# Two 1024x1024 products as seven half-size products each, from sums of operand quadrants

## The chip, the cores and the metric

The kernel runs on one core of one Trainium2 chip. The metric is the device time of one execution in microseconds (us), the median of several executions. In the profile PE is TensorE (the matmuls), PEld its weight loads, DVE is VectorE, ACT is ScalarE, POOL is GpSimd and SP is the engine from whose queue nearly all DMAs are issued.

## The reference, cut to what matters

One layer of an encoder on 1024 tokens of width 1024. Four mixers (a linear recurrence, neighbourhood attention, a state-space model and a pooling mixer) give four branches of width 512; the change touches what comes behind them, the last two 1024x1024 products.

```python
ys = jnp.stack([y_a, y_b, y_c, y_d], axis=2).astype(x.dtype)
gates = jax.nn.sigmoid(merge.reshape(bsz, s, N_BRANCH, D_MODEL))
merged = jnp.sum(jnp.einsum('bsnw,nwd->bsnd', ys, w_branch[i]) * gates, axis=2)
x = x + (merged @ w_out[i]).astype(x.dtype)
x = x + jax.nn.sigmoid(x @ ple_gate[i]) * (p[i] @ ple_proj[i])
```

All of `merged`, `w_out`, `x` and `ple_gate` are 1024x1024 in float32. `p @ ple_proj` is computed early and lies in DRAM as `pp`.

## The kernel before

Every large product is made of three matmuls per block: an operand is split into a high part H (a ScalarE copy, rounded to the type fp32r) and a low part L = operand - H (a VectorE subtraction), and H·H + H·L + L·H are summed in PSUM (`split`, L83; `mm3`, L87, whose three matmuls are L92 to L94). One matmul has a 128x128 stationary and a 128x512 moving operand. A 1024x1024x1024 product therefore takes 8 (contraction chunks) x 8 (token tiles) x 2 (column halves) x 3 = 384 matmuls.

The order on each engine is made by a scheduler when the kernel is built; at run time each engine works through its own queue in that order, and an instruction that waits holds up all that stand behind it on that engine. DMAs of the SP queue are issued in order too.

`merge` (L1174) goes through the four branches in the order 1, 0, 2, 3. For each branch it makes 8 row tiles m of 128 features by 1024 tokens, each in two halves of 512 tokens (PSUM tiles `ps_s` and `ps_o`, two buffers each). VectorE multiplies the PSUM half by the gate (`mgt`, read from DRAM, four buffers) and adds it to the accumulator `acc` (two instructions of 128x512). In the last branch the sum goes back into `mgt`, and whenever a row tile is complete it is split into `mH` and `mL`, which lie where the normed input lay.

`final` (L1200) then runs four blocks: two column halves of the product with `w_out`, two of the product with `ple_gate`. Each block loads its weights (`wide_load`, two tiles `wr` of 1 MB), splits them (`wide_split`, four pieces of 128x1024) and makes 8 token tiles of 24 matmuls (`wide_product`, PSUM `ps_z`, two buffers). `put_x` adds the input to a token tile (`fx`), stores it to DRAM as `x1d`, transposes it with four matmuls against the identity (`ps_t`, L97), and splits it into `xH`, `xL`, the operand of the second product. `put_o` takes the sigmoid, multiplies by `pp`, adds `x1d` and stores the output.

Of the kernel before, what the change touches and what calls it, by code (L numbers as in the profile page):

```python
# [24 lines left out]
BANDS = (0, 8, 24, 32)  # L25
SC = (1.25, 1.35, 0.95)
VIDX = (0, 1, 1, 2)


class Kern:  # L30
# [308 lines left out]

    def norm_load(self, tmp, hf):  # L340
        if hf == 0:
            self.hnH = [self.big.tile([128, 1024], F32R, tag=f"bH{k}", name="hnH") for k in range(8)]
            self.hnL = [self.big.tile([128, 1024], F32R, tag=f"bL{k}", name="hnL") for k in range(8)]
# [167 lines left out]
    def at_units(self, ap, rd, qk, bias, vd):  # L511
# [9 lines left out]
        for g in range(2):  # L521
# [14 lines left out]
            for j in range(4):  # L536
# [597 lines left out]

    def y_split(self, yp, mp, n, out):

        hl = [[yp.tile([128, 1024], F32R, tag=f"my{k}{j}", name="my" + "HL"[j]) for j in range(2)]
              for k in range(4)]
        yield 0.0, 0.0
        for k in range(4):  # L1140
            y = mp.tile([128, 1024], F32, tag="mgt", name="my", bufs=4)
            self.nc.sync.dma_start(y, self.yd[n][k * 128:k * 128 + 128, :])
            if n == 1:
                g = mp.tile([128, 1024], F32, tag="mgt", name="myg", bufs=4)
                self.nc.sync.dma_start(g, self.sgd[1][k * 128:k * 128 + 128, :])
                self.mul(y, y, g)
            H, L = hl[k]
            self.split(H, L, y)
            out.append((H, L))
            yield 0.0, 2.0  # L1150
# [21 lines left out]
                    yield m, hf, gt, pb  # L1172

    def merge(self, mp, mq, order, Y):  # L1174
        acc = [self.big.tile([128, 1024], F32, tag=f"bH{k}", name="acc") for k in range(8)]
        self.mH, self.mL = [], []
        for a, n in enumerate(order):
            nxt = []
            pre = self.y_split((mp, mq)[(a + 1) % 2], mp, order[a + 1], nxt) if a < 3 else iter(())
            for m, hf, gt, pb in self.branch_products(mp, n, Y):  # L1180
                t = slice(hf * 512, hf * 512 + 512)
                if a == 0:
                    self.mul(acc[m][:, t], pb, gt[:, t])
                else:
                    self.mul(gt[:, t], pb, gt[:, t])
                    if a < 3:
                        self.add(acc[m][:, t], acc[m][:, t], gt[:, t])
                    else:
                        self.add(gt[:, t], acc[m][:, t], gt[:, t])
                        if hf:  # L1190
                            H, L = (self.big.tile([128, 1024], F32R, tag=f"b{c}{m}", name=f"m{c}") for c in "HL")
                            self.split(H, L, gt)
                            self.mH.append(H)
                            self.mL.append(L)
                if m >= 2 and hf:
                    next(pre, None)
            Y = nxt


    def final(self):  # L1200
        nc, i = self.nc, self.i
        x1d = self.dp.tile([S, D], F32, name="x1d")
        mH, mL = self.mH, self.mL
        with self.tc.tile_pool(name="fn", bufs=2, reuse_waits="tile") as fp:
            xH = fp.tile([128, 8, 1024], F32R, name="xH", bufs=1)
            xL = fp.tile([128, 8, 1024], F32R, name="xL", bufs=1)

            def put_x(nb, t, ps):
                cols, tk = slice(nb * 512, nb * 512 + 512), slice(t * 128, t * 128 + 128)
                x = fp.tile([128, 512], F32, tag="fx", name="fx", bufs=3)  # L1210
                nc.sync.dma_start(x, i["x"][tk, cols])
                yield
                self.add(x, x, ps())
                nc.sync.dma_start(x1d[tk, cols], x)
                pt = self.ps("t")
                for c in range(4):
                    self.tr(pt[:, c * 128:c * 128 + 128], x[:, c * 128:c * 128 + 128], 128)
                k = slice(nb * 4, nb * 4 + 4)
                self.split(xH[:, k, tk], xL[:, k, tk], pt.rearrange("p (c q) -> p c q", c=4))

            def put_o(nb, t, ps):
                cols, tk = slice(nb * 512, nb * 512 + 512), slice(t * 128, t * 128 + 128)
                o = fp.tile([128, 512], F32, tag="fx", name="fo", bufs=3)
                nc.sync.dma_start(o, x1d[tk, cols])
                pw = fp.tile([128, 512], F32, tag="fp", name="fp")
                nc.sync.dma_start(pw, self.pp[tk, cols])
                yield
                g = fp.tile([128, 512], F32, tag="fg", name="fg")
                self.act(g, ps(), AF.Sigmoid)
                self.mul(g, g, pw)  # L1230
                self.add(o, o, g)
                nc.sync.dma_start(self.out[0][tk, cols], o)

            self.fw = itertools.count()
            blocks = [(n, nb) for n in ("w_out", "ple_gate") for nb in range(2)]
            raws = [self.wide_load(*blocks[0])]
            for m, (n, nb) in enumerate(blocks):
                if m < 2:
                    self.wide_product(fp, [a[:, :] for a in mH], [a[:, :] for a in mL], raws[0], put_x, nb)
                else:  # L1240
                    self.wide_product(fp, [xH[:, k, :] for k in range(8)], [xL[:, k, :] for k in range(8)],
                                      raws[0], put_o, nb)
                raws = [self.wide_load(*blocks[m + 1])] if m < 3 else []

    def wide_load(self, n, nb):

        out = []
        for kh in range(2):
            r = self.wp.tile([128, 4, 512], F32, tag="wr", name="wr")
            self.nc.sync.dma_start(r, self.i[n][kh * 512:kh * 512 + 512, nb * 512:nb * 512 + 512]  # L1250
                                   .rearrange("(k p) n -> p k n", p=128))
            out.append(r)
        return out

    def wide_split(self, fp, raws):
        hl = []
        for q in range(4):
            if next(self.fw) % 5 < 3:
                H, L = self.whl([128, 2, 512])
            else:  # L1260
                H, L = (fp.tile([128, 2, 512], F32R, tag="fw" + c, name="w" + c) for c in "hl")
            self.split(H, L, raws[q // 2][:, q % 2 * 2:q % 2 * 2 + 2, :])
            hl += [(H[:, k, :], L[:, k, :]) for k in range(2)]
        return hl

    def wide_product(self, fp, aH, aL, raws, put, nb):

        hl = self.wide_split(fp, raws)
        box = [None]
        nxt = put(nb, 0, lambda: box[0])  # L1270
        next(nxt)
        for t in range(8):
            cur = nxt
            ps = self.ps("z")
            c = slice(t * 128, t * 128 + 128)
            self.mm3(ps, [(aH[k][:, c], aL[k][:, c]) + hl[k] for k in range(8)])
            if t < 7:
                nxt = put(nb, t + 1, lambda: box[0])
                next(nxt)
            box[0] = ps  # L1280
            next(cur, None)

    def run(self):
        tc = self.tc
        with tc.tile_pool(name="gzp", bufs=2, reuse_waits="tile") as self.gzp:
# [13 lines left out]
            with tc.tile_pool(name="mp", bufs=1, reuse_waits="tile") as mp:  # L1299
# [9 lines left out]
            self.final()  # L1309


def encoder_kernel(tc, ins, out):
# [33 lines left out]
```

## Time and profile before

| | |
|---|---|
| time before, median of 3 runs | 1386.07 us (1385.12 to 1386.26) |
| the profiled execution: its own time | 1385.52 us |
| the profiled execution: its span | 1383.7 us |
| busy TensorE, share of the span | 99% |
| busy VectorE | 61% |
| busy ScalarE | 38% |
| granted TensorE clock, mean | 0.999 |

The span is that of the instructions in the trace; the execution's own time has 1.82 us more around it. Positions in the program are given in us from the start of the span.

### The profile page before, as it was taken

To read this page: it belongs to the slowest core of one execution; us is meant where nothing else is said; L and a number is where in the kernel's file an instruction comes from. 1 tells how busy PE (TensorE), PEld (TensorE's weight loads), DVE (VectorE), ACT (ScalarE), POOL (GpSimd) and SP (SyncE) were. 2 spreads that over 40 slices of the span, in tenths; PEclk is the share of its full clock that TensorE was granted. 3 is DMA by queue.
4 is the path that set the end of the run, shared out by engine and by line. 5 is a ranking of instruction groups with operands and counts; after the bars stand their busy time and mean duration, and the time that the engine had idled before them with its cause. 6 is when DMAs were issued, how large, how long until landed. Compare 5 with 4: busy or idle time off the path is not lost.

```text
span 1383.7 us, 19208 instructions
## 1 busy us (share of the span) xinstructions
PE 1368.5 (99%) x7450; PEld 1159.6 (84%) x7450; DVE 843.8 (61%) x1592; ACT 521.3 (38%) x825; POOL 20.6 (1%) x81
## 2 busy tenths in 40 slices
PE   7999999999999999999999999999999999999998
PEld 6999998888788888788888888888888888888886
DVE  6551766455299797979757556636566767732332
ACT  6542676588332222222243662644312212211211
POOL 2200000000000000000000000000000000000000
PEclk9999999999999999999999999999999999999999
DMA  9451223433443142324264143135527655333543
GB/s 323 130 146 59 72 77 118 133 105 109 100 127 99 61 129 89 114 88 127 91 213 142 35 140 110 61 137 188 213 94 258 206 175 176 135 108 128 179 144 119
DMA packets 141054, 181.99 MB, mean 132 GB/s; under 512 B 29200, under 2 KB 100888, under 8 KB 140962
## 3 DMA queue, kind: packets, MB, share of 16 engines
q1 hardware_dynamic: 140610, 180.72, 40.4%
q8 instruction: 59, 0.97, 0.3%
q14 instruction: 33, 0.27, 0.1%
q0 software_dynamic: 352, 0.03, 0.0%
HBM read 127.05 MB, written 54.03 MB: 131 GB/s over the span
## 4 chain that ended last, share of the span: by engine, by line
PE 93%; DVE 5%; DMA 1%; ACT 1%; issue 0%; SPq 0%; DVEq 0%
PE ps_z L92 19%; PE ps_z L93 19%; PE ps_z L94 19%; PE ps_t L97 4%; PE ps_t L93 4%; PE ps_t L92 4%; PE ps_t L94 4%; PE ps_o L92 3%; PE ps_o L93 3%; PE ps_o L94 3%; PE ps_s L92 3%; PE ps_s L93 3%; PE ps_s L94 3%; PE ps_o L578 2%; PE ps_s L543 2%; PE ps_s L1068 1%
## 5 line engine op out<-in xcount | busy, mean ns | idle before, releaser
L92 PE MATMUL ps_z<-hnH,wh 128*128 128x512 f32 x744 | 293.2, 394 | 2.0 <-DVE bgt L58 2.0
L93 PE MATMUL ps_z<-hnL,wh 128*128 128x512 f32 x744 | 292.0, 392 | 0.0
L94 PE MATMUL ps_z<-hnH,wl 128*128 128x512 f32 x744 | 291.9, 392 | 0.0
L64 DVE TENSOR_TENSOR wl<-wr,wh 128x1024 fp32r<-128x1024 f32 x88 | 107.4, 1221 | 110.4 <-ACT wh L80 109.6
L92 PEld LDWEIGHTS ps_z<-hnH,wh 128*128 128x128 f32 x744 | 139.8, 188 | 30.8 <-DVE bgt L58 2.4
L94 PEld LDWEIGHTS ps_z<-hnH,wl 128*128 128x128 f32 x744 | 139.8, 188 | 28.5 <-issue 0.4
L93 PEld LDWEIGHTS ps_z<-hnL,wh 128*128 128x128 f32 x744 | 139.8, 188 | 27.9 <-issue 0.4
L80 ACT ACTIVATE wh<-wr 128x1024 fp32r<-128x1024 f32 x88 | 93.0, 1059 | 166.3 <-PE ps_z L93 81.2
L92 PE MATMUL ps_z<-wh,hnH 128*128 128x256 f32 x384 | 108.3, 285 | 0.5 <-ACT zqk L80 0.5
L94 PE MATMUL ps_z<-wh,hnL 128*128 128x256 f32 x384 | 108.5, 287 | 0.0
L93 PE MATMUL ps_z<-wl,hnH 128*128 128x256 f32 x384 | 108.1, 283 | 0.0
L93 PE MATMUL ps_t<-hnL,wh 128*128 128x512 f32 x216 | 84.2, 390 | 0.0
L92 PE MATMUL ps_t<-hnH,wh 128*128 128x512 f32 x216 | 84.1, 389 | 0.0
L94 PE MATMUL ps_t<-hnH,wl 128*128 128x512 f32 x216 | 84.0, 389 | 0.0
L92 PEld LDWEIGHTS ps_z<-wh,hnH 128*128 128x128 f32 x384 | 73.2, 192 | 1.2 <-ACT zqk L80 1.2
L93 PEld LDWEIGHTS ps_z<-wl,hnH 128*128 128x128 f32 x384 | 73.5, 191 | 0.0
L94 PEld LDWEIGHTS ps_z<-wh,hnL 128*128 128x128 f32 x384 | 72.9, 192 | 0.0
L94 PE MATMUL ps_z<-wh,mL 128*128 128x512 f32 x128 | 51.0, 399 | 0.0
L549 DVE CUSTOM_DVE_ANT_0 sc<-ps_s,bias 128x384 f32<-128x384 f32 x64 | 34.2, 554 | 27.2 <-PE ps_s L543 14.6
L92 PE MATMUL ps_o<-myH,wh 128*128 128x512 f32 x128 | 49.9, 390 | 0.4 <-DVE pm L67 0.4
L92 PE MATMUL ps_z<-wh,mH 128*128 128x512 f32 x128 | 50.2, 393 | 0.0
L93 PE MATMUL ps_z<-wl,mH 128*128 128x512 f32 x128 | 50.0, 391 | 0.0
(371 smaller groups left out, 2596.9 us busy)
## 6 DMA issues: line engine op xcount, KB each, us to landing
wr<-in_w_in_dram SPq DMA_DIRECT2D x32, 1024.0 KB, 5.3
gd<-gz SPq DMA_DIRECT2D x32, 512.0 KB, 2.9
mgt<-gd SPq DMA_DIRECT2D x32, 512.0 KB, 4.2
sg<-bgt SPq DMA_DIRECT2D x16, 512.0 KB, 3.1
my<-yd SPq DMA_DIRECT2D x16, 512.0 KB, 4.2
mbr<-in_w_branch_dram SPq DMA_DIRECT2D x8, 1024.0 KB, 6.7
bias<-E SPq DMA_DIRECT2D x128, 48.0 KB, 2.0
xt<-in_x_dram SPq DMA_DIRECT2D x8, 512.0 KB, 10.0
```

The lines of the kernel that those rows point to most:

```text
L64: self.nc.vector.tensor_tensor(out, a, b, ALU.subtract)
L80: return self.nc.scalar.activation(out, a, AF.Copy)
L92: mm(ps, aH, bH, start=(k == 0), stop=False)
L93: mm(ps, aH, bL, start=False, stop=False)
L94: mm(ps, aL, bH, start=False, stop=(k == n - 1))
L97: self.nc.tensor.transpose(ps, src, self.ident[:k, :k])
L543: nc.tensor.matmul(pss[h], q[h][:, qs], km[h][(slice(0, 128),) + ks], start=(p == 0), stop=(p == 1))
L549: nc.vector.tensor_tensor_reduce(sc, pss[h], bias[g][h][:, VIDX[j], :], 1.0, -3e38, ALU.add, ALU.max, mx)
L578: m = self.nc.tensor.matmul(po[64 * h:64 * h + 64, j * 128:j * 128 + 128], vb[:, g + c, j, h * 64:h * 64 + 64], PT[h][:, c * 128:c * 128 + ...
L1068: nc.tensor.matmul(py[:, c], Q[k][:, a, 1:9, :].rearrange("p t c -> p (t c)"), X[k][:, c], start=False, stop=(k == 1))
```

## The change

The two last products are computed by a seven-product scheme instead of the plain one. The left operand A (1024 tokens by 1024) and the weights B are cut into quadrants of 512x512. Seven products of 512x512x512 are made from sums and differences of quadrants, and the four quadrants of the result are sums of these seven. A half-size product has 4 (contraction chunks) x 4 (token tiles) x 3 = 48 matmuls of the same shape as before.

- `merge` no longer splits its result: the accumulator `m` (128x8x1024, float32) stays whole. At the start of the last branch the four quadrants of `w_out` (`wq`, 1 MB each) are loaded into the buffers from which the third branch read its left operand (`my`).
- `seven` runs the seven products. `prep` makes the operands of the next one while the present one runs: per half of the contraction a sum or difference of the left quadrants (into `stmp` or back into `m`), its split into `ah`, a difference of weight quadrants (in place), and its split into `wh`, `wl`. The numbers 1 to 7 are the keys of `plan`.
- Products 1, 6, 7 and 4 add up in one set of four PSUM tiles (X), 5 and 3 and then 2 in another (Z). After products 1, 6 and 5 ScalarE copies the sum so far to `snap` tiles in SBUF. After products 3, 7, 2 and 4 a quadrant of the result is complete: `put_x` or `put_o` adds the snapshot and the PSUM tile.
- `put_x` still stores `x1d` and transposes, but ScalarE copies the result unsplit into `m`, in the place of a quadrant that is no longer needed (`QPOS`). Loads of the input go into four buffers `fx`, which `put_o` also uses for reading `x1d` back.
- The quadrants of `ple_gate` (`gq`) are loaded around the end of `merge`.
- The normed input and each branch's left operand become one tile per group in place of one per chunk; every instruction up to the last branch stands where it stood.

```diff
+QPOS = {(0, 1): (0, 0), (1, 1): (0, 1), (0, 0): (1, 0), (1, 0): (1, 1)}
...
-            self.hnH = [self.big.tile([128, 1024], F32R, tag=f"bH{k}", name="hnH") for k in range(8)]
+            hn = [self.big.tile([128, 8, 1024], F32R, tag="b" + c, name="hn" + c) for c in "HL"]
...
-        acc = [self.big.tile([128, 1024], F32, tag=f"bH{k}", name="acc") for k in range(8)]
+        self.m = self.big.tile([128, 8, 1024], F32, tag="bH", name="m")
...
+            if a == 3:
+                self.raw = [mp.tile([128, 4, 512], F32, tag=f"my{q}", name="wq") for q in range(4)]
+                for q in range(4):
+                    self.quadrant("w_out", q, self.raw[q])
...
-                            H, L = (self.big.tile([128, 1024], F32R, tag=f"b{c}{m}", name=f"m{c}") for c in "HL")
-                            self.split(H, L, gt)
...
+                    self.add(acc, acc, gt[:, t])
...
+            ah = self.big.tile([128, 4, 2, 2, 512], F32R, tag="bL", name="ah")
+            self.ah = [[ah[:, q, j] for j in range(2)] for q in range(4)]
+            self.stmp = fp.tile([128, 4, 512], F32, name="stmp")
+            self.snap = [fp.tile([128, 4, 512], F32, name=f"snap{k}") for k in range(3)]
+            gate = [self.wp.tile([128, 4, 512], F32, tag="wr", name="gq") for _ in range(2)]
+            gate += [fp.tile([128, 4, 512], F32, name=f"gq{q}") for q in range(2)]
+            for q in (0, 2, 1, 3):
+                self.quadrant("ple_gate", q, gate[q])
...
+            def put_x(t, nb, part, ps, x, tag):
+                if part is not None:
+                    self.add(x, x, part)
+                self.add(x, x, ps)
+                pt = self.ps(tag)
...
+                self.copy_a(self.m[:, 4 * kq:4 * kq + 4, tq * 512 + t % 4 * 128:tq * 512 + t % 4 * 128 + 128],
+                            pt.rearrange("p (c q) -> p c q", c=4))
...
+            def load_o(t, nb):
+                o = fp.tile([128, 512], F32, tag="fx", name="fo", bufs=4)
+                pw = mp.tile([128, 512], F32, tag="mgt", name="pw", bufs=4)
+                return o, pw
...
+            def put_o(t, nb, part, ps, opw, tag):
+                o, pw = opw
+                g = part if part is not None else self.snap[0][:, t - 4, :]
+                if part is not None:
+                    self.add(g, part, ps)
+                    self.act(g, g, AF.Sigmoid)
+                else:
+                    self.act(g, ps, AF.Sigmoid)
...
+            home = {(r, c): (c, r) for r in range(2) for c in range(2)}
+            first = self.seven(home, self.raw, (1, 5, 6, 3, 7, 2, 4), ("zztt", "ssoo"), load_x, put_x)
+            second = self.seven(QPOS, gate, (1, 2, 5, 6, 3, 7, 4), ("ssoo", "zztt"), load_o, put_o)
+            next(first)
+            for _ in range(6):
+                next(first)
+            next(second)
+            for _ in first:
+                pass
+            for _ in second:
+                pass
...
+        def A(r, c):
+            kq, tq = pos[r, c]
+            return self.m[:, 4 * kq:4 * kq + 4, tq * 512:tq * 512 + 512]
+        B11, B12, B21, B22 = (raw[q] for q in range(4))
+        st, (s1, s2, z5) = self.stmp, self.snap
+        A11, A12, A21, A22 = A(0, 0), A(0, 1), A(1, 0), A(1, 1)
+
+        plan = {1: ((), (), A11, B11),
+                5: (((st, A21, A22, ALU.add),), ((B11, B12, B11, ALU.subtract),), st, B11),
+                6: (((st, st, A11, ALU.subtract),), ((B11, B22, B11, ALU.subtract),), st, B11),
+                3: (((st, A12, st, ALU.subtract),), (), st, B22),
+                7: (((A21, A11, A21, ALU.subtract),), ((B12, B22, B12, ALU.subtract),), A21, B12),
+                2: ((), (), A12, B21),
+                4: ((), ((B11, B21, B11, ALU.subtract),), A22, B11)}
+
+        def prep(p):
+            sa, sb, a, b = plan[p]
+            out = []
+            for h in range(2):
+                k = slice(2 * h, 2 * h + 2)
+                for o, x, y, op in sa:
+                    self.tt(o[:, k], x[:, k], y[:, k], op)
+                aH, aL = self.ah[next(self.fa) % 4]
+                self.split(aH, aL, a[:, k])
+                for o, x, y, op in sb:
+                    self.tt(o[:, k], x[:, k], y[:, k], op)
+                bH, bL = self.bchunk()
+                self.split(bH, bL, b[:, k])
+                out.append((aH, aL, bH, bL))
+            return out
+        X, Z = [None] * 4, [None] * 4
+        ready = prep(order[0])
+        yield
+        for n, p in enumerate(order):
+            aux = [None] * 4
+            tok, nb = {3: (0, 1), 7: (4, 1), 2: (0, 0), 4: (4, 0)}.get(p, (0, 0))
+            if p in (3, 7, 2, 4):
+                aux = [load(tok + g, nb) for g in range(4)]
+            now = ready
+            if n + 1 < 7:
+                ready = prep(order[n + 1])
+            for g in range(4):
+                if p == 1:
+                    X[g] = self.ps(tags[0][g])
+                elif p in (5, 2):
+                    Z[g] = self.ps(tags[1][g])
+            acc = X if p in (1, 6, 7, 4) else Z
+            for h, (aH, aL, bH, bL) in enumerate(now):
+                for g in range(4):
+                    c = slice(g * 128, g * 128 + 128)
+                    for k in range(2):
+                        begin = h == 0 and k == 0 and p in (1, 5, 2)
+                        end = h == 1 and k == 1
+                        mm = self.nc.tensor.matmul
+                        mm(acc[g], aH[:, k, c], bH[:, k, :], start=begin, stop=False, skip_group_check=True)
+                        mm(acc[g], aH[:, k, c], bL[:, k, :], start=False, stop=False, skip_group_check=True)
+                        mm(acc[g], aL[:, k, c], bH[:, k, :], start=False, stop=end, skip_group_check=True)
+            for g in range(4):
+                if p == 1:
+                    self.copy_a(s1[:, g, :], X[g])
+                elif p == 5:
+                    self.copy_a(z5[:, g, :], Z[g])
+                elif p == 6:
+                    self.copy_a(s2[:, g, :], X[g])
                 else:
+                    part = {3: s2, 7: z5, 2: s1, 4: None}[p]
+                    put(tok + g, nb, part if part is None else part[:, g, :], acc[g], aux[g],
+                        tags[0][g] if p == 4 else tags[1][g])
+            yield
+
+    def bchunk(self):
+        if next(self.fb) % 4 < 3:
+            return self.whl([128, 2, 512])
+        return tuple(self.gzp.tile([128, 2, 512], F32R, tag="gz", name="w" + c) for c in "hl")
```

In the rows below, two line numbers higher means the same helper: L63 is the add of L61, L66 the subtraction of `split`, L57 the new sums, L99 the transposes, L1326 to L1328 the three matmuls of `seven`. Rows are as the build orders them, one queue at a time.

The first place is the SP queue at the start of the last branch, whose gates are `gd_87`. Before:

```order
L1166 DMA mgt<-gd_88 128x1024
L1166 DMA mgt<-gd_87 128x1024 x2
L1250 DMA wr<-in_w_out_dram 128x4x512
L1166 DMA mgt<-gd_87 128x1024 x3
L1250 DMA wr<-in_w_out_dram 128x4x512
L1166 DMA mgt<-gd_87 128x1024 x3
L1250 DMA wr<-in_w_out_dram 128x4x512
```

The same place in the changed kernel:

```order
L1168 DMA mgt<-gd_88 128x1024
L1168 DMA mgt<-gd_87 128x1024 x2
L1201 DMA gq<-in_ple_gate_dram 128x4x512
L1168 DMA mgt<-gd_87 128x1024
L1201 DMA wq<-in_w_out_dram 128x4x512 x4
L1168 DMA mgt<-gd_87 128x1024 x3
L1201 DMA gq<-in_ple_gate_dram 128x4x512
L1168 DMA mgt<-gd_87 128x1024 x2
```

Four loads of 1 MB now stand together ahead of the gates of the fourth to eighth row tile, and they wait for the last matmuls of the third branch, which read the buffers they fill.

The second place is VectorE where the first product ends and the second begins. Before (`xL` is the low half of the transposed result):

```order
L61 TENSOR_TENSOR fx<-fx,ps_z 128x512
L64 TENSOR_TENSOR xL<-ps_t,xH 128x4x128
L61 TENSOR_TENSOR fx<-fx,ps_z 128x512
L64 TENSOR_TENSOR xL<-ps_t,xH 128x4x128
L61 TENSOR_TENSOR fx<-fx,ps_z 128x512
```

The changed kernel, from the last addition of product 2's result to the low half of the left operand of the second product's product 1 (the tenth row; the row with x2 holds the next low halves):

```order
L63 TENSOR_TENSOR fx<-fx,ps_o 128x512
L66 TENSOR_TENSOR wl<-gq,wh 128x1024
L66 TENSOR_TENSOR ah<-m,ah 128x1024
L57 TENSOR_TENSOR gq<-gq 128x1024
L63 TENSOR_TENSOR fx<-fx,ps_z 128x512
L66 TENSOR_TENSOR wl<-gq_10824,wh 128x1024
L63 TENSOR_TENSOR fx<-fx,ps_z 128x512
L57 TENSOR_TENSOR gq<-gq_10825,gq 128x1024
L63 TENSOR_TENSOR fx<-fx,ps_t 128x512
L66 TENSOR_TENSOR ah<-m,ah 128x1024
L63 TENSOR_TENSOR fx<-fx,ps_t 128x512
L66 TENSOR_TENSOR ah<-m,ah 128x1024 x2
```

Between two additions of a finished token tile there now stand operand sums and splits of 128x1024.

The third place is TensorE at the same seam, between the last product of `w_out` and the first of `ple_gate`. Before:

```order
L92 MATMUL ps_z<-wh,mH 128x512
L93 MATMUL ps_z<-wl,mH 128x512
L97 MATMUL ps_t<-ident,fx 128x128 x4
L94 MATMUL ps_z<-wh,mL 128x512
L92 MATMUL ps_z<-wh,xH 128x512
```

The changed kernel (`ps_s`, `ps_o` are the first product of `ple_gate`; the transposes are those of the last quadrant of the first result; here the names carry buffer numbers, so that the four token tiles can be told apart):

```order
L99 MATMUL ps_z_11444<-ident_69,fx_11386 128x128 x4
L1326 MATMUL ps_s_11486<-wh_11376,ah_10817 128x512
L1327 MATMUL ps_s_11486<-wl_11377,ah_10817 128x512
L1326 MATMUL ps_s_11487<-wh_11376,ah_10817 128x512
L1327 MATMUL ps_s_11487<-wl_11377,ah_10817 128x512
L1326 MATMUL ps_o_11488<-wh_11376,ah_10817 128x512
L1327 MATMUL ps_o_11488<-wl_11377,ah_10817 128x512
L1326 MATMUL ps_o_11489<-wh_11376,ah_10817 128x512
L1327 MATMUL ps_o_11489<-wl_11377,ah_10817 128x512
L99 MATMUL ps_z_11452<-ident_69,fx_11388 128x128 x4
L99 MATMUL ps_t_11460<-ident_69,fx_11390 128x128 x4
L1328 MATMUL ps_s_11486<-wh_11376,ah_10817 128x512
```

Only eight matmuls, those that use the high half of the left operand, stand before the transposes; the first that uses the low half (L1328) stands behind three groups of transposes.

## Rows read from the trace of the kernel before

**Rows 1.** The page's busy times, the granted clock in 40 slices, and its last chain.

```profile
PE 1368.5 (99%) x7450; PEld 1159.6 (84%) x7450; DVE 843.8 (61%) x1592; ACT 521.3 (38%) x825; POOL 20.6 (1%) x81
...
PEclk9999999999999999999999999999999999999999
...
PE 93%; DVE 5%; DMA 1%; ACT 1%; issue 0%; SPq 0%; DVEq 0%
```

**Rows 2.** Busy time by stretch: last branch, product with `w_out`, product with `ple_gate`.

```profile
core 0: us, PE busy (x) PEld busy (x) DVE busy (x) ACT busy (x) POOL busy (x), PEclk, DMA share, GB/s
1150.00:1196.50 46.50, 46.50 (x206) 38.50 (x206) 35.35 (x45) 11.69 (x11) 0.00 (x0) 1.00 0.46 159
1196.50:1290.90 94.40, 94.40 (x445) 77.97 (x444) 32.64 (x42) 19.84 (x25) 0.00 (x0) 1.00 0.35 116
1290.90:1378.50 87.60, 87.60 (x389) 72.28 (x388) 28.01 (x38) 14.31 (x21) 0.00 (x0) 1.00 0.47 158
```

**Rows 3.** TensorE in order of time, inside a block: start, duration, instruction.

```profile
1330.24 0.39 PE L92 MATMUL ps_z<-wh,xH 128*128 128x512 f32 x1
1330.47 0.39 PE L93 MATMUL ps_z<-wl,xH 128*128 128x512 f32 x1
1330.70 0.39 PE L94 MATMUL ps_z<-wh,xL 128*128 128x512 f32 x1
1330.92 0.39 PE L92 MATMUL ps_z<-wh,xH 128*128 128x512 f32 x1
```

**Rows 4.** TensorE in order of time, where the second product begins.

```profile
1290.04 0.39 PE L93 MATMUL ps_z<-wl,mH 128*128 128x512 f32 x1
1290.27 0.60 PE L97 MATMUL ps_t<-ident,fx 128*128 128x128 f32 x4
1290.63 0.48 PE L94 MATMUL ps_z<-wh,mL 128*128 128x512 f32 x1
1290.94 0.40 PE L92 MATMUL ps_z<-wh,xH 128*128 128x512 f32 x1
```

**Rows 5.** All engines in order of time, the end of the program.

```profile
1378.30 0.39 PE L94 MATMUL ps_z<-wh,xL 128*128 128x512 f32 x1
1378.72 0.60 ACT L76 ACTIVATE fg<-ps_z 128x512 f32<-128x512 f32 x1 [4.84 <-PE ps_z L94]
1379.35 0.69 DVE L58 TENSOR_TENSOR fg<-fg,fp 128x512 f32<-128x512 f32 x1 [4.02 <-ACT fg L76]
1380.08 0.69 DVE L61 TENSOR_TENSOR fo<-fo,fg 128x512 f32<-128x512 f32 x1
```

**Rows 6.** Groups of instructions by shape behind 1100 us: count, busy, mean ns, idle before.

```profile
L64 DVE TENSOR_TENSOR wl<-wr,wh 128x1024 fp32r<-128x1024 f32 x16 | 19.5, 1223 | 8.2 <-ACT wh L80 7.6
L61 DVE TENSOR_TENSOR fx<-fx,ps_z 128x512 f32<-128x512 f32 x16 | 11.0, 686 | 55.5 <-PE ps_z L94 55.5
...
L80 ACT ACTIVATE wh<-wr 128x1024 fp32r<-128x1024 f32 x16 | 16.9, 1059 | 18.0 <-PE ps_o L93 8.3 <-DMA wr<-in_ple_gate_dram 5.0 <-PE ps_z L94 4.7
L80 ACT ACTIVATE xH<-ps_t 128x512 fp32r<-128x512 f32 x16 | 9.6, 599 | 68.1 <-PE ps_t L97 68.1
```

**Rows 7.** DMA issues behind 1050 us: count, KB each, median us to landing.

```profile
wr<-in_w_out_dram SPq DMA_DIRECT2D x4, 1024.0 KB, 4.8
fx<-in_x_dram SPq DMA_DIRECT2D x16, 256.0 KB, 2.9
...
x1d<-fx SPq DMA_DIRECT2D x16, 256.0 KB, 2.4
...
fo<-x1d SPq DMA_DIRECT2D x16, 256.0 KB, 2.6
out_dram<-fo SPq DMA_DIRECT2D x16, 256.0 KB, 2.7
```

**Rows 8.** The SP queue in order of time around the start of the last branch.

```profile
1147.28 0.38 SPq L1250 DMA_DIRECT2D wr<-in_w_out_dram  x1
1149.93 13.59 SPq L1166 DMA_DIRECT2D mgt<-gd  x3
```

**Rows 9.** Busy time in a stretch full of loads; the last column is GB/s.

```profile
1192.00:1196.00 4.00, 4.00 (x19) 3.34 (x18) 2.70 (x4) 1.06 (x1) 0.00 (x0) 1.00 1.03 381
```

More of the change, by code (lines that the diff above doesn't have):

```diff
@@ L341, in norm_load @@
         if hf == 0:
-            self.hnH = [self.big.tile([128, 1024], F32R, tag=f"bH{k}", name="hnH") for k in range(8)]
-            self.hnL = [self.big.tile([128, 1024], F32R, tag=f"bL{k}", name="hnL") for k in range(8)]
+            hn = [self.big.tile([128, 8, 1024], F32R, tag="b" + c, name="hn" + c) for c in "HL"]
+            self.hnH, self.hnL = ([a[:, k, :] for k in range(8)] for a in hn)
         x = self.i["x"]
@@ L1135, in y_split @@
     def y_split(self, yp, mp, n, out):
-        hl = [[yp.tile([128, 1024], F32R, tag=f"my{k}{j}", name="my" + "HL"[j]) for j in range(2)]
-              for k in range(4)]
+        hl = [yp.tile([128, 2, 1024], F32R, tag=f"my{k}", name="my") for k in range(4)]
+        hl = [(a[:, 0, :], a[:, 1, :]) for a in hl]
         yield 0.0, 0.0
@@ L1174, in merge @@
     def merge(self, mp, mq, order, Y):
-        acc = [self.big.tile([128, 1024], F32, tag=f"bH{k}", name="acc") for k in range(8)]
-        self.mH, self.mL = [], []
+        self.m = self.big.tile([128, 8, 1024], F32, tag="bH", name="m")
         for a, n in enumerate(order):
@@ L1179, in merge @@
             pre = self.y_split((mp, mq)[(a + 1) % 2], mp, order[a + 1], nxt) if a < 3 else iter(())
+            if a == 3:
+                self.raw = [mp.tile([128, 4, 512], F32, tag=f"my{q}", name="wq") for q in range(4)]
+                for q in range(4):
+                    self.quadrant("w_out", q, self.raw[q])
             for m, hf, gt, pb in self.branch_products(mp, n, Y):
                 t = slice(hf * 512, hf * 512 + 512)
+                acc = self.m[:, m, t]
                 if a == 0:
-                    self.mul(acc[m][:, t], pb, gt[:, t])
+                    self.mul(acc, pb, gt[:, t])
                 else:
                     self.mul(gt[:, t], pb, gt[:, t])
[L1186 to L1190, printed above, removed]
-                            H, L = (self.big.tile([128, 1024], F32R, tag=f"b{c}{m}", name=f"m{c}") for c in "HL")
-                            self.split(H, L, gt)
-                            self.mH.append(H)
-                            self.mL.append(L)
+                    self.add(acc, acc, gt[:, t])
                 if m >= 2 and hf:
@@ L1197, in merge, with quadrant, final, load_x @@
             Y = nxt
-    def final(self):
+    def quadrant(self, n, q, out):
+        r, c = q // 2 * 512, q % 2 * 512
+        self.nc.sync.dma_start(out, self.i[n][r:r + 512, c:c + 512].rearrange("(k p) n -> p k n", p=128))
+    def final(self, mp):
         nc, i = self.nc, self.i
         x1d = self.dp.tile([S, D], F32, name="x1d")
[L1203 to L1208, printed above, removed]
+        with self.tc.tile_pool(name="fn", bufs=1, reuse_waits="tile") as fp:
+            self.fp, self.fa, self.fb = fp, itertools.count(), itertools.count()
+            ah = self.big.tile([128, 4, 2, 2, 512], F32R, tag="bL", name="ah")
[6 more added lines that the diff above has]
+                self.quadrant("ple_gate", q, gate[q])
+            def load_x(t, nb):
+                x = fp.tile([128, 512], F32, tag="fx", name="fx", bufs=4)
+                nc.sync.dma_start(x, i["x"][t * 128:t * 128 + 128, nb * 512:nb * 512 + 512])
+                return x
+            def put_x(t, nb, part, ps, x, tag):
@@ L1209, in put_x @@
                 cols, tk = slice(nb * 512, nb * 512 + 512), slice(t * 128, t * 128 + 128)
[L1210 to L1213, printed above, removed]
+                if part is not None:
+                    self.add(x, x, part)
+                self.add(x, x, ps)
                 nc.sync.dma_start(x1d[tk, cols], x)
-                pt = self.ps("t")
+                pt = self.ps(tag)
@@ L1216, in put_x @@
                 for c in range(4):
                     self.tr(pt[:, c * 128:c * 128 + 128], x[:, c * 128:c * 128 + 128], 128)
-                k = slice(nb * 4, nb * 4 + 4)
-                self.split(xH[:, k, tk], xL[:, k, tk], pt.rearrange("p (c q) -> p c q", c=4))
-            def put_o(nb, t, ps):
+                kq, tq = QPOS[t // 4, nb]
+                self.copy_a(self.m[:, 4 * kq:4 * kq + 4, tq * 512 + t % 4 * 128:tq * 512 + t % 4 * 128 + 128],
+                            pt.rearrange("p (c q) -> p c q", c=4))
@@ L1228, in put_o @@
-                g = fp.tile([128, 512], F32, tag="fg", name="fg")
-                self.act(g, ps(), AF.Sigmoid)
+                return o, pw
[7 more added lines that the diff above has]
+                    self.act(g, ps, AF.Sigmoid)
@@ L1230, in put_o @@
                 self.mul(g, g, pw)
                 self.add(o, o, g)
[L1232 to L1239, printed above, removed]
-                else:
-                    self.wide_product(fp, [xH[:, k, :] for k in range(8)], [xL[:, k, :] for k in range(8)],
-                                      raws[0], put_o, nb)
-                raws = [self.wide_load(*blocks[m + 1])] if m < 3 else []
@@ L1245, in wide_load @@
[L1245 to L1281, printed above, removed]
+                nc.sync.dma_start(self.out[0][t * 128:t * 128 + 128, nb * 512:nb * 512 + 512], o)
@@ new lines, in final, with seven @@
+            home = {(r, c): (c, r) for r in range(2) for c in range(2)}
[9 more added lines that the diff above has]
+                pass
+    def seven(self, pos, raw, order, tags, load, put):
+        def A(r, c):
[60 more added lines that the diff above has]
+                    self.copy_a(s2[:, g, :], X[g])
+                else:
+                    part = {3: s2, 7: z5, 2: s1, 4: None}[p]
+                    put(tok + g, nb, part if part is None else part[:, g, :], acc[g], aux[g],
+                        tags[0][g] if p == 4 else tags[1][g])
+            yield
@@ L1308, in run @@
                     self.merge(mp, mq, (1, 0, 2, 3), Y)
-            self.final()
+                self.final(mp)
 def encoder_kernel(tc, ins, out):
```

3 lines of the change are left out of this document (removed).

## The prediction, on record before the run

> **What bounds the kernel now.** I began with the page's busy times and its last chain: TensorE is busy for 1368.5 us of 1383.7, and 93% of the chain that ended last is its own [rows 1]. The windows then show the three stretches in question: last branch, product with `w_out`, product with `ple_gate`. In each TensorE is busy for the whole stretch, at a granted clock of 1.00, while VectorE has 35.35 of 46.5, 32.64 of 94.4 and 28.01 of 87.6 us and GpSimd nothing [rows 2]. So behind 1150 us the time is the sum of TensorE's instructions, and a matmul taken out shortens the program by its slot, unless another engine now comes too late with an operand.
>
> The slot is read from starts, not durations, since the ends are modelled: (1330.92 - 1330.24) / 3 = 0.2267 us [rows 3]. Four transposes and one matmul take 1290.94 - 1290.27 = 0.67 us [rows 4], so a group of four transposes costs 0.67 - 0.2267 = 0.44 us. As a check, the first product is 384 x 0.2267 + 16 x 0.44 = 94.1 us, and its window has 94.4; the second is 87.0, and its window has 87.6 [rows 2].
>
> **What is removed.** Seven products of 48 matmuls are 336 in place of 384. Twice 48 is 96 matmuls x 0.2267 = 21.8 us. All 64 transposes stay (16 groups, 7.0 us). The tail from 1196.5 to the last matmul falls from 182.0 to 182.0 - 21.8 = 160.2 us. The rule that speaks against this size: the Trainium skill, page "TensorE: Matmul & The Clock Gate", section "Wait — 56ns, not 53.3ns?", gives a start-to-start of columns / 2.4 GHz + 2.5 ns, 215.7 ns at 512 columns; by it the 96 matmuls are worth an estimated 20.7 us. The row says 226.7 ns, 11 ns more, and the sum goes by the row.
>
> **What is added, and what hides it.** Behind the last addition of `merge` VectorE gets 76 instructions of 128x1024 (operand sums, low halves) and 72 of 128x512 (additions of results, sigmoid products). A 128x1024 subtraction with both inputs in SBUF takes 1.223 us and a 128x512 addition 0.686 [rows 6]: 92.9 + 49.4 = 142.3 us against the 160.2 us of TensorE. ScalarE gets 50 of 128x1024 and 56 of 128x512 (high halves, snapshots, copies of transposes, sigmoids): 50 x 1.059 + 56 x 0.599 = 86.5 us [rows 6]. Both fit, VectorE at 89% of the stretch in place of a third. What the work costs is therefore decided at hand-overs, where TensorE waits for one operand. I walked the changed queues row by row with these durations:
>
> - Start of `w_out`: in the last 24.5 us of `merge` VectorE has 11 wide and 20 narrow instructions, 27.2 us of work, but product 1's operands come early in that row, and product 5's are due a whole product (48 x 0.2267 = 10.9 us) later. About 4 us are left over. No cost.
> - Inside the products the other hand-overs have 1 to 5 us left, but for the tightest below and one of about 0.5 us (product 5 to 6 of the second). No cost, but little cover: one narrow instruction more takes it there.
> - The seam between the products. From the end of product 2's first PSUM tile until the low half of the next left operand, VectorE has 9 wide and 7 narrow: 11.0 + 4.8 = 15.8 us. TensorE has 56 matmuls and 7 groups of transposes before it needs that half: 12.7 + 3.1 = 15.8 us. That leaves nothing for VectorE's start behind the last matmul, so L1328 waits. The bounds are 0 (VectorE starts at once) and 4 us (three wide instructions further back); I take 0.3, nearest to the row count.
> - Seam through DRAM: a result row is stored as `x1d` in 2.4 us and the `fx` buffer is filled again in 2.9 us [rows 7]. With four buffers some 1.4 us remain. No cost.
>
> The four loads of `w_out` (4.19 MB) now stand in the SP queue ahead of the gates of row tiles four to eight, and wait for the third branch's last matmuls. Before, single loads stood between the gates, at 1147.28 and 1149.93 [rows 8]. A branch is 192 matmuls, so the last starts at 1196.5 - 192 x 0.2267 = 1153.0, and the loads go out a little later, at some 1155. VectorE needs the fourth tile's gate at 1153.0 + 3 x 5.44 + 2.72 = 1172 (24 matmuls a tile, 5.44 us); with two PSUM buffers TensorE waits only if it has not come by 1180.2. At 381 GB/s, which a crowded stretch reached [rows 9], the burst and the gate behind it (0.52 MB) take 12.4 us, to 1167.4. One load after the other at 4.8 us [rows 7] is 19.2 us, and the gate lands near 1176, with 4 us to spare. I take no cost; the other end is in a rival.
>
> The end. Before, the last matmul starts at 1378.30, and a sigmoid of 0.60 and two VectorE instructions of 0.69 follow until 1380.08 + 0.69, then the store [rows 5]. This stays. New is that the last tile's `x1d` is read into a buffer that must first be stored: out 2.7, in 2.6 [rows 7]. Most of that lies under the last product's 10.9 us. Bounds 0 and 5.3 us; I take 0.7, since three of the four buffers come free in time.
>
> **The sum.** Span 1383.7 - 21.8 + 0.3 + 0.7 = 1362.9. The profiled execution's own time, 1385.52, has 1.82 us around its span: 1364.7. The median of the runs, 1386.07, is 0.55 above that execution, so the forecast for a median is **1365.3 us**, 0.985 of before. A measurement of this kernel can tell some 0.2% (2.8 us) from no change.
>
> **The rivals.**
> - *The burst holds up the last branch.* If DMA gives the loads only the 159 GB/s that the last branch drew [rows 2], they and the gate take 4.71 / 0.159 = 29.6 us, to 1184.6: a stall of 4.4 us, **1370**. It decides below 4.71 MB / (1180.2 - 1155) = 187 GB/s. For it: the other gates run at the same time. Against: 381 GB/s was drawn without a pause of TensorE [rows 9].
> - *The chain of hand-overs slips.* VectorE's queue is in order, and a result's addition waits for TensorE with operand work behind it. If each of the 12 changes of product inside the two schemes is late by one narrow or one wide instruction (0.69 to 1.22 us [rows 6]), that is 8 to 15 us: **1374**, at worst 1380. For it: 89% of an engine with waits in its queue. Against: the row-by-row walk, in which most hand-overs have more than one instruction left.
> - *VectorE becomes the bound, and the kernel slower.* The 76 wide instructions read quadrants, that is pieces of 512 with gaps between. If these take w us each, VectorE's tail is 76 w + 49.4 (142.3 at 1.223), and exceeds the old 182.0 from w = 1.745 on; slower by 2.8 us from w = 1.78. At 1.9 it is 193.8, **1398**. Against: whole-tile subtractions take 1.223, and the wide rows have 16 alike [rows 6]; GpSimd is idle [rows 2].
> - *The clock falls.* Where TensorE pauses at each hand-over its granted clock could go from 2.4 to 1.2 GHz, and a product run so costs 48 x 0.2267 = 10.9 us more: one such product gives **1376**. Against: all 40 slices are at 9 [rows 1], all stretches at 1.00 [rows 2], where TensorE hardly pauses. The Trainium skill has this mechanism on the page "TensorE: Matmul & The Clock Gate", section "A second HAM failure mode: psum-queue depth-cycling": frequent short idles between groups of matmuls while PSUM is cycled made the clock swing. No row here shows it.
> - *It brings nothing.* If the matmul slot rises from 0.2267 to 0.259 us, because VectorE, ScalarE and TensorE now use SBUF together all the time, 672 x 0.0325 = 21.8 us are lost again: **1386**. Against: in the last branch VectorE was already busy for three quarters of the time, and TensorE did 206 instructions, transposes none, in 46.5 us: 0.226 each [rows 2].
>
> **How the numbers follow.** Chances: the forecast 0.71 (its own range 1363 to 1368, from the bounds of its two small stalls and a slot of a per mille less), the slipping chain 0.15, the burst 0.06, VectorE as the bound 0.03, no gain 0.03, the clock 0.02. The likeliest case gives 1365.3. The range 1363 to 1374 holds the forecast, the burst and the better half of the slipping chain, 0.84 in all. Faster by over 0.2% are the forecast, burst, slip and clock, 0.94; within 0.2% 0.03; slower 0.03.
>
> **What the changed profile would show.** Right: 672 matmuls behind the last branch at 0.2267 us, TensorE idle for under 1 us ahead of L1328 at the seam and nowhere else, VectorE busy for some 140 us of the last 160, the four `wq` loads landing by 1176 with no pause of TensorE in the last branch, clock 9 in all slices, some 3 us from the last matmul to the end of VectorE. Wrong: pauses of TensorE ahead of L1326 or L1328 with VectorE as the releaser (slip); a pause ended by a multiplication behind `mgt` between 1170 and 1190 (burst); means of the 128x1024 rows over 1.5 us (VectorE); starts of matmuls more than 0.23 us apart (slot).

## The result, and the profile after

The changed kernel takes 1368.29 us (median of four runs, 1365.96 to 1368.79) against 1385.88 before in the same comparison: a ratio of 0.987, with an interval of 0.9853 to 0.9888. The forecast was 1365.3, its range 1363 to 1374. The profiled execution has a span of 1366.2 us, where 1362.9 was forecast.

The page of the changed kernel: busy times, the granted clock in slices, and its last chain (before in [rows 1]).

```profile
PE 1346.5 (99%) x7354; PEld 1142.2 (84%) x7354; DVE 918.9 (67%) x1664; ACT 565.0 (41%) x881; POOL 20.9 (2%) x81
...
PEclk9999999999999999999999999999999999999998
...
PE 92%; DVE 5%; DMA 1%; issue 1%; ACT 0%; SPq 0%; DVEq 0%
```

TensorE has 22.0 us less work. VectorE has 75 us more, and is not in the chain any more than before. The 8 in the clock's last slice lies where TensorE is mostly idle, behind its last matmul. The windows of the last branch, most of the first product, the rest up to the last matmuls, and the end (before in [rows 2]):

```profile
core 0: us, PE busy (x) PEld busy (x) DVE busy (x) ACT busy (x) POOL busy (x), PEclk, DMA share, GB/s
...
1150.00:1196.50 46.50, 46.50 (x207) 38.48 (x206) 35.26 (x45) 7.43 (x7) 0.00 (x0) 1.00 0.59 211
1196.50:1276.50 80.00, 80.00 (x378) 66.51 (x377) 64.33 (x70) 39.66 (x51) 0.00 (x0) 1.00 0.34 120
1276.50:1361.00 84.50, 80.33 (x363) 66.24 (x361) 70.53 (x83) 42.52 (x57) 0.00 (x0) 0.99 0.44 143
1361.00:1366.20 5.20, 0.00 (x0) 0.00 (x0) 1.45 (x3) 0.00 (x0) 0.00 (x0) 0.50 0.46 174
```

In the first two rows TensorE has no idle time; in the third it has 84.50 - 80.33 = 4.2 us, which lie behind its last matmul. No hand-over stalls it. The changed kernel in order of time (start, duration, instruction; in brackets the idle time before it and what ended it): the first two matmuls of the first product, the place where the second product begins, VectorE inside the second, and the end.

```profile
1196.94 0.39 PE L1326 MATMUL ps_z<-wh,ah 128*128 128x512 f32 x1
1197.17 0.39 PE L1327 MATMUL ps_z<-wl,ah 128*128 128x512 f32 x1
...
1279.37 1.22 DVE L66 TENSOR_TENSOR ah<-m,ah 128x1024 fp32r<-128x1024 f32 x1
...
1281.73 0.48 PE L1328 MATMUL ps_s<-wh,ah 128*128 128x512 f32 x1
...
1316.67 1.22 DVE L66 TENSOR_TENSOR ah<-stmp,ah 128x1024 fp32r<-128x1024 f32 x1
1317.80 1.22 DVE L66 TENSOR_TENSOR wl<-gq,wh 128x1024 fp32r<-128x1024 f32 x1
1318.94 1.22 DVE L66 TENSOR_TENSOR ah<-stmp,ah 128x1024 fp32r<-128x1024 f32 x1
...
1334.61 0.68 DVE L63 TENSOR_TENSOR snap<-snap,ps_t 128x512 f32<-128x512 f32 x1
1335.21 0.68 DVE L63 TENSOR_TENSOR fo<-fo,snap 128x512 f32<-128x512 f32 x1
...
1351.41 0.69 DVE L63 TENSOR_TENSOR fo<-fo,snap 128x512 f32<-128x512 f32 x1 [0.68 <-DMA fo<-x1d]
1352.67 0.32 SPq L1238 DMA_DIRECT2D fo<-x1d  x1
1353.08 0.38 SPq L1253 DMA_DIRECT2D out_dram<-fo  x1
1353.56 0.39 SPq L1238 DMA_DIRECT2D fo<-x1d  x1
1354.04 0.45 SPq L1253 DMA_DIRECT2D out_dram<-fo  x1
1356.44 0.39 PE L1328 MATMUL ps_o<-wh,ah 128*128 128x512 f32 x1
1356.75 0.69 DVE L63 TENSOR_TENSOR fo<-fo,snap 128x512 f32<-128x512 f32 x1 [4.65 <-DMA fo<-x1d]
1356.87 0.60 ACT L78 ACTIVATE snap<-ps_o 128x512 f32<-128x512 f32 x1 [0.76 <-PE ps_o L1328]
...
1362.53 0.69 DVE L63 TENSOR_TENSOR fo<-fo,snap 128x512 f32<-128x512 f32 x1 [0.77 <-DMA fo<-x1d]
```

The two products last 1356.44 - 1196.94 = 159.5 us from the first matmul's start to the last one's; before it was 1378.30 [rows 5] - 1196.5 [rows 2] = 181.8. That is 22.3 us less. But from the last matmul's start to the start of the last addition it is 1362.53 - 1356.44 = 6.09 us, where it was 1380.08 - 1378.30 = 1.78 [rows 5]. So 4.3 us are given back at the end, by what is called the end below: the time from the last matmul's start to the last addition's start. The chain that ended last says by what it grew:

```profile
1354.04 4.52 DMA out_dram<-fo
...
1358.57 3.83 DMA fo<-x1d
...
1362.53 0.69 DVE fo L63
```

The last addition of product 7 ends at 1351.41 + 0.69 = 1352.10, but its store goes out at 1354.04, 1.94 us later: it stands in the SP queue behind a read (1352.67) and a store (1353.08) and one more read (1353.56). It lands after 4.52 us; only then can the same buffer `fo` be filled with the `x1d` of product 4's last tile, 3.83 us more; only then comes the last addition. The sigmoid was done at 1356.87 + 0.60 = 1357.47, five microseconds earlier.

The span is 3.3 us over the forecast one, and the parts account for 3.2 of them. The end grew by 6.09 - 1.78 = 4.3 where 0.7 was forecast: +3.6. The products became 22.3 us shorter where 21.8 - 0.3 = 21.5 was forecast: -0.8. And the first product starts 0.4 later.

### The profile page after: what moved, and what is told of

The parts are those of the page before. It is cut to its first block, busy times and chain, and to the rows that moved or that the text cites. A ratio compares the mean times of both kernels' runs of the same rounds, so it can differ in the third digit from the quotient of the medians.

```text
span 1366.2 us, 19163 instructions
## 1 busy us (share of the span) xinstructions
PE 1346.5 (99%) x7354; PEld 1142.2 (84%) x7354; DVE 918.9 (67%) x1664; ACT 565.0 (41%) x881; POOL 20.9 (2%) x81
## 4 chain that ended last, share of the span: by engine, by line
PE 92%; DVE 5%; DMA 1%; issue 1%; ACT 0%; SPq 0%; DVEq 0%
PE ps_z L94 15%; PE ps_z L95 15%; PE ps_z L96 15%; PE ps_t L96 4%; PE ps_t L95 4%; PE ps_t L94 4%; PE ps_t L99 3%; PE ps_o L94 3%; PE ps_o L96 3%; PE ps_o L95 3%; PE ps_s L94 3%; PE ps_s L96 3%; PE ps_s L95 3%; PE ps_o L580 2%; PE ps_s L545 2%; PE ps_z L1326 1%
## 5 line engine op out<-in xcount | busy, mean ns | idle before, releaser
L66 DVE TENSOR_TENSOR wl<-wr,wh 128x1024 fp32r<-128x1024 f32 x72 | 88.0, 1222 | 101.2 <-ACT wh L82 101.1
L82 ACT ACTIVATE wh<-wr 128x1024 fp32r<-128x1024 f32 x72 | 76.1, 1059 | 148.6 <-PE ps_z L95 81.1
L94 PE MATMUL ps_o<-my,wh 128*128 128x512 f32 x128 | 49.9, 390 | 0.4 <-DVE pm L69 0.4
L78 ACT ACTIVATE gz<-ps_z 128x512 f32<-128x512 f32 x45 | 26.7, 593 | 56.9 <-issue 35.1
L94 PE MATMUL ps_s<-my,wh 128*128 128x512 f32 x128 | 49.8, 389 | 0.0
L96 PE MATMUL ps_s<-my,wl 128*128 128x512 f32 x128 | 49.8, 389 | 0.0
```

The lines of the kernel that those rows point to most:

```text
L66: self.nc.vector.tensor_tensor(out, a, b, ALU.subtract)
L78: self.nc.scalar.activation(out, a, f, **kw)
L82: return self.nc.scalar.activation(out, a, AF.Copy)
L94: mm(ps, aH, bH, start=(k == 0), stop=False)
L96: mm(ps, aL, bH, start=False, stop=(k == n - 1))
```

## The experiments

The theory: the sum of TensorE's instructions sets the time up to the last matmul, and the miss is the end, where the `fo` buffers go through store and read in turn. In e1, e2 and e8 the instructions on TensorE, VectorE and ScalarE stand in the order of the changed kernel; in e3, e4, e6 and e7 the scheduler also moved neighbours.

**e1: the last four reads into other buffers.**

```diff
-                o = fp.tile([128, 512], F32, tag="fx", name="fo", bufs=4)
+                if t >= 4 and nb == 0:
+                    o = self.stmp[:, t - 4, :]
+                else:
+                    o = fp.tile([128, 512], F32, tag="fx", name="fo", bufs=4)
```

> The x1d tiles of the last product go into stmp, which is free by then, in place of the four fo buffers that must first be stored; the order on TensorE, VectorE and ScalarE stays. My theory (the program ends late because a reload waits for the store of the same buffer): the last addition follows the last sigmoid product at once, 1.8 us behind the start of the last matmul as in the kernel before, not 6.1; the span falls by 4.3 to some 1361.9, the median to some 1364. Rival (the stores and reads at the end are limited by DMA itself, whatever the buffers): within 1 us of the changed kernel, 1367.5 to 1369.

Measured: 1363.39 us (1363.04 to 1364.05), ratio to before 0.9843 (0.9828 to 0.9857), span 1361.4. The end of e1 in order of time:

```profile
1355.82 0.39 PE L1331 MATMUL ps_o<-wh,ah 128*128 128x512 f32 x1
...
1357.60 0.69 DVE L63 TENSOR_TENSOR stmp<-stmp,snap 128x512 f32<-128x512 f32 x1
```

1357.60 - 1355.82 = 1.78 us, as before the change. The 4.3 us are gone, and they are shown to come from the `fo` buffers' turn of store and read, with all that a read waiting for its buffer holds up. e1 is faster than both kernels.

**e2: the reads in a queue of their own.**

```diff
-                nc.sync.dma_start(o, x1d[tk, cols])
+                nc.gpsimd.dma_start(o, x1d[tk, cols])
```

> Same four fo buffers, but the sixteen reads of x1d are issued from GpSimd's queue, so that no store in the SP queue stands behind a read that waits. If the cost is the order of the SP queue (a waiting read holds up the stores behind it): a store goes out at the end of its addition, the last chain is store 4.5 + read 3.8 from 1352.1, the last addition near 1361 or earlier, and the median falls by 1.5 to 4 us, to 1364.5 to 1367. If it is the number of buffers alone: within 1 us of the changed kernel. If GpSimd issues DMAs slowly: slower, 1369 or more.

Measured: 1367.79 (1367.27 to 1368.93), the same as the changed kernel. The last chain of e2:

```profile
1353.57 3.71 DMA out_dram<-fo
...
1357.31 0.04 POOLq L1238
1357.35 0.57 issue
...
1357.94 3.16 DMA fo<-x1d
...
1361.80 0.69 DVE fo L63
```

The store and the read of one buffer still follow each other, and the end is 6.35 us (1361.80 less 1355.45, where the last matmul starts). The store now goes out when its addition ends, at 1353.54, so the 1.94 us that it stood in the SP queue in the changed kernel are gone. But product 7's last addition itself comes later: 156.9 us behind the first matmul, where it was 154.5 in the changed kernel. And a read from GpSimd's queue has its own delay, 0.65 us from the store's landing at 1357.28 to 1357.94. So a queue of its own for the reads is no remedy. How much of the 4.3 us the order of the SP queue has in the changed kernel is not shown: e2 trades it against a slower start of the reads, and e1 takes away the turn and the waiting reads at once.

**e3 and e4: eight half-size products in the new structure**, for the second product alone and for both. The unsplit `m`, the quadrants, the splits in halves and the pools stay; the operand sums go, and each result quadrant is two plain half-size products in one set of PSUM tiles. In e4 the transposed tiles of the first result overwrite quadrants that its later products still read; the work is all there. The edit of the second product, cut (e4 replaces `first` in the same way):

```diff
-            second = self.seven(QPOS, gate, (1, 2, 5, 6, 3, 7, 4), ("ssoo", "zztt"), load_o, put_o)
+            second = self.eight(QPOS, gate, ("ssoo", "zztt"), load_o, put_o)
...
+        out = [(0, 1), (1, 1), (0, 0), (1, 0)]
+        steps = [(r, c, k) for r, c in out for k in range(2)]
```

> The second product by eight half-size products in the same structure (unsplit m, quadrants, same buffers and pools), the first still by seven. My theory (the gain is 48 matmuls a product at 0.2267 us, and TensorE never waits): 1368.3 + 10.9 = 1379.2, within 1.5. Rival (the new structure itself gains or costs several us): more than 3 us away from that.

> Both products by eight half-size products in the same structure, so nothing of the 96 matmuls is saved. My theory: 1368.3 + 21.8 = 1390.1, that is slower than the kernel before by the longer end of the program, some 4 us, and by nothing else. Rival (the structure costs as much as it saves elsewhere): 1386, no different from the kernel before; or a stall on TensorE at hand-overs, over 1392.

Measured: e3 1374.29 (1373.29 to 1375.59), e4 1386.32 (1385.71 to 1386.64), ratio of e4 to before 1.0005 (0.9996 to 1.0015). Both are some 4 to 5 us under what I expected. I had carried the slow end over to them, and it isn't there. The end of e3 in order of time:

```profile
1368.34 0.39 PE L1379 MATMUL ps_t<-wh,ah 128*128 128x512 f32 x1
...
1370.12 0.69 DVE L63 TENSOR_TENSOR fo<-fo,snap 128x512 f32<-128x512 f32 x1
```

Again 1.78 us. With eight products a quadrant of the result comes only with every second product, so an `fo` buffer has two products' time for its store and read; with seven the last two quadrants come from the last two products, 10.9 us apart. That is my reading of the order; behind 1300 us VectorE waits for no read of `x1d` in e3 and e4. Against e1, which has the short end too, the steps agree: 1374.29 - 1363.39 = 10.9 us for 48 matmuls, 1386.32 - 1363.39 = 22.9 for 96, where the matmul slot of 0.2267 us gives 10.9 and 21.8. In e4 TensorE waits once, for a copy of the transposed result:

```profile
PE ps_s L1377 <- ACT m L82: 0.6, 1, 0.6
```

Otherwise the new structure costs nothing that shows in the time.

**e5: the changed kernel again**, for comparison with e6 to e8.

> The changed kernel once more, beside the next three: within 0.2% of its 1368.3, with a pause of over 4 us on VectorE near the end that a read of x1d ends.

Measured: 1367.9 (1367.75 to 1369.32). Its products last 159.5 us too and its end 6.97; the first matmul starts 1.1 us earlier than in the first profile of the same kernel. Over all profiles of these experiments it starts between 1195.8 and 1198.0.

**e6 and e7: more work on VectorE.** The subtraction that makes the weights' low half is done a second time, with the same result. e6 does it for the first half of each product's weights, as shown; e7 does it for both halves, without the `if`.

```diff
                 self.split(bH, bL, b[:, k])
+                if h == 0:
+                    self.sub(bL, b[:, k], bH.bitcast(F32))
```

> The low half of the first weight half of each product is subtracted twice, 14 instructions of 128x1024 more, by 1.14 to 1.22 us each 16 to 17 us: VectorE's work behind the last branch is then 158 to 159 us against TensorE's 160.2. My theory (cover is decided at each hand-over, and the tight ones have under 1.2 us left): TensorE pauses at several L1326 or L1328 rows and the time rises by 1 to 6 us, to 1369 to 1374. Rival (only the sum counts, and it still fits): 1368.3 as the changed kernel. Rival (TensorE never depends on this work closely): 1368.3 too, and also in the next run.

> Both low halves of the weights of each product are subtracted twice: 28 more, 32 to 34 us, VectorE's work 174 to 176.5 us against TensorE's 160.2. My theory: VectorE is now the bound, the time rises by at least 14 to 16 us, to 1382 to 1390, nearly back to the kernel before, with TensorE paused at most products. Rival (VectorE's work is off the path whatever its sum): 1368.3.

Measured: e6 1376.49 (1376.15 to 1377.66), 8.6 over e5; e7 1383.84 (1381.43 to 1385.94), 15.9 over e5. What TensorE waited for in e6 (in total, times, longest):

```profile
PE ps_z L1329 <- DVE wl L66: 1.5, 2, 1.3
PE ps_s L99 <- DVE fx L63: 1.2, 1, 1.2
```

And in e7:

```profile
PE ps_s L1328 <- DVE wl L66: 4.0, 1, 4.0
PE ps_s L99 <- DVE fx L63: 2.7, 1, 2.7
PE ps_s L1327 <- ACT ah L82: 1.3, 1, 1.3
PE ps_z L1327 <- DVE snap L63: 0.3, 1, 0.3
```

The sums fail as a criterion. VectorE's 128x1024 instructions start 1.13 to 1.14 us apart when nothing holds them (1317.80 - 1316.67 in the first timeline above; 1.136 in the mean of some 70 such pairs), and its 128x512 instructions 0.60. So its work in the changed kernel is about 76 x 1.136 + 72 x 0.60 = 129.5 us, in e6 145.4 and in e7 161.3, against 159.5 of TensorE. By the sum e6 would have lost nothing and e7 2 us. TensorE's stretch from first to last matmul became 164.2 in e6 (4.7 more) and 173.6 in e7 (14.1 more). VectorE's spare time lies in waits of its own. The longest of the changed kernel (in total, times, longest), and what ScalarE waits for ahead of them:

```profile
ACT ah L82 <- PE ps_t L1327: 15.1, 9, 3.4
...
DVE ah L66 <- ACT ah L82: 9.7, 7, 2.7
...
DVE fx L63 <- DMA fx<-in_x_dram: 6.5, 7, 1.6
```

VectorE waits for high halves, ScalarE waits with these until TensorE has read the `ah` buffer, and reads of the input come late. Such a pause can't be used for instructions that stand further behind in the queue; that this is why the sums fail is argued, not tested.

My theory held for the kind of stall, and not for its size. e6 lies above its range of 1369 to 1374. The end, which I had left out, grew by 2.4 us (9.33 in place of 6.97), as the stores and reads start later; the waits shown are 2.7 of the 4.7 us of the stretch, the rest is not attributed; and the first matmul started 1.7 later. That e7 lies in its range is luck: its 14 to 16 us were a sum of durations over TensorE's stretch, of which the sum of starts leaves 2. The profiled execution of e7, the longest of ten, has a span 18.2 us over e5's: 14.1 in the stretch, of which 8.3 are the waits shown and some 4 are a lower clock behind two of them (last section), and 4.2 in the end (11.12 in place of 6.97).

**e8: the burst doubled.**

```diff
-                for q in range(4):
+                for q in (0, 1, 2, 3, 0, 1, 2, 3):
                     self.quadrant("w_out", q, self.raw[q])
```

> Each quadrant of w_out is loaded twice, 8.4 MB in place of 4.2 at the start of the last branch, the second four loads between the gates of the fifth to seventh row tile. My theory (the burst is hidden with at least 8 us to spare at the measured landing of the fourth gate): no pause of TensorE before the products, 1368.3. Rival (the loads were hidden by little): a pause of 3 us or more in the last branch or at the first operands of product 1, 1371 or more.

Measured: 1369.1 (1368.77 to 1370.23), 0.1% over e5, less than can be told from no change. The last branch of e8:

```profile
1150.00:1196.50 46.50, 46.50 (x207) 38.52 (x206) 34.90 (x45) 7.43 (x7) 0.00 (x0) 1.00 0.80 302
```

302 GB/s in the mean, and TensorE busy throughout. In the changed kernel itself the four loads go out from 1151.6 to 1153.8 and land after 6.6 to 10.9 us, so by 1164.7.

## Why the prediction was right, and which term was off

The time fell as forecast because a TensorE that never waits loses 96 slots; that the median came out 3.0 us above the forecast is nearly all one term, the end. Going through the terms:

- *TensorE's sum.* Right. Forecast -21.8 us for 96 matmuls; the stretch fell by 22.3, and 10.9 us for one product of 48 came back in e3. The slot of 0.2267 us [rows 3] held (1197.17 - 1196.94 = 0.23 above), so the rival of a longer slot is out. The half microsecond beyond 21.8 doesn't come from the matmuls saved: e4 has as many as before, and its stretch of 182.0 without the wait of 0.6 is 181.4, against 181.8. What in the new order gives it is not settled.
- *VectorE hidden.* Right, and with more room than I gave it: I summed durations (1.223 and 0.686 [rows 6]), but back to back the instructions start 1.136 and 0.60 apart. e6 shows how little room is left all the same. My "No cost" for the input read into a buffer that had to be stored first, with 1.4 us left, holds for TensorE only: VectorE waited seven times for such reads, 6.5 us in all.
- *The seam between the products, 0.3 us.* Not there. By starts VectorE needs 9 x 1.136 + 7 x 0.60 = 14.4 us, not 15.8. The low half is done at 1279.37 + 1.22 = 1280.59, and L1328 starts at 1281.73, 1.1 us later and without a pause ahead of it.
- *The burst, no cost.* Right, with room for twice the bytes (e8).
- *The end, 0.7 us.* The term that was mis-sized: 4.3 us, within its bounds of 0 to 5.3. The step that failed is "I take 0.7, since three of the four buffers come free in time". All four buffers are in the same position: product 7's tiles are finished 10.9 us before product 4's, and their additions are spread over 1345.84 to 1351.41. And the turn of a buffer was mis-sized: the last took 1.94 us in the queue, 4.52 for the store and 3.83 for the read, 10.3 us in all, where I had 2.7 and 2.6 [rows 7]. With 0.7 replaced by 4.3 the forecast would have been 1368.9.
- *The rivals.* The slipping chain and the fallen clock needed TensorE to pause, and it didn't; e6 shows the first with 14 instructions more, e7 both with 28. VectorE as the bound needed 128x1024 instructions of 1.745 us or more; on quadrants they took 1.216 to 1.222 us in the mean.

## What to carry to other kernels

TensorE was busy here without a gap, and the work taken off it came back in full, at its slot read from starts. The engine that takes over the work is to be judged hand-over by hand-over, that is operand by operand, and not by its sum: here 81% by the sum cost TensorE nothing, and 91% (e6) already 4.7 us. And look behind the last instruction of the bound engine: a shorter last stage leaves less time for buffers that go out and come in again, and a scratch tile that is free by then can take the last reads.

## What the runs showed of the hardware

The clock rival appeared in e7, where it was not sought. Windows of e7 around its longest pause, and its matmuls behind it:

```profile
1326.00:1330.60 4.60, 0.58 (x3) 0.16 (x1) 4.60 (x6) 1.71 (x2) 0.00 (x0) 0.86 0.66 225
1330.60:1336.00 5.40, 5.40 (x13) 4.23 (x14) 5.40 (x5) 1.19 (x2) 0.00 (x0) 0.50 0.31 99
1336.00:1346.00 10.00, 10.00 (x45) 8.28 (x44) 9.45 (x10) 5.57 (x7) 0.00 (x0) 0.99 0.00 0
```

```profile
1330.60 0.79 PE L1328 MATMUL ps_s<-wl,ah 128*128 128x512 f32 x1 [4.02 <-DVE wl L66]
1331.20 0.63 PE L1329 MATMUL ps_s<-wh,ah 128*128 128x512 f32 x1
...
1335.46 0.63 PE L1329 MATMUL ps_o<-wh,ah 128*128 128x512 f32 x1
```

TensorE had been idle for 4.0 us, waiting for VectorE; behind that its granted clock is 0.50, that is 1.2 GHz, and the ten slots from 1331.20 to 1335.46 are 0.426 us each, against 0.2267 at 2.4 GHz. Thirteen matmuls so run cost some 13 x 0.20 = 2.6 us, a seventh of this execution's loss, on top of the pause. The Trainium skill gives 426.7 ns for this slot at the lower clock (page "TensorE: Matmul & The Clock Gate", section "Wait — 56ns, not 53.3ns?"), and the trace agrees. The same stands behind e7's second pause:

```profile
1256.37 0.63 PE L99 MATMUL ps_s<-ident,fx 128*128 128x128 f32 x4 [2.66 <-DVE fx L63]
...
1258.28 0.63 PE L1329 MATMUL ps_z<-wh,ah 128*128 128x512 f32 x1
1258.71 0.63 PE L1327 MATMUL ps_z<-wh,ah 128*128 128x512 f32 x1
```

From 1256.40 to 1261.00 the granted clock is 0.63 in the mean, and these starts are 0.43 apart; summed over the starts up to 1261.17 that costs an estimated 1.5 us. In e6 the longest wait of TensorE was 1.3 us, and the windows around it stay at 1.00. So a late operand can cost more than its lateness.
